# Two stick-breaking heads side by side on the array, and three small jobs handed to GpSimd

## The chip, the core and the metric

The kernel runs on one core of one Trainium2 chip. The metric is the device time of one execution in microseconds (us), as the median of several runs. The core has five queues that run on their own and meet through semaphores: TensorE (PE, matrix products), VectorE (DVE), ScalarE (ACT), GpSimd (POOL) and SyncE (SP, which issues most loads). Each executes its instructions strictly in the order in which they were built.

## What is computed

The reference is one layer of a hybrid decoder for 256 tokens of width 2048. The change touches the token mixer, the first of three sub-layers. The mixer projects its input once and splits the result into three groups:

- a diagonal state space model (S5) over 512 channels,
- eight stick-breaking attention heads of 64 channels,
- sixteen NSA attention heads (compressed, selected and window keys) that share a relative position bias.

Stick-breaking, cut to what matters:

```python
z = einsum('bqhd,bkhd->bhqk', qb, k) * scale
log1m = where(mask, log_sigmoid(-z), 0.0)
later = cumsum(log1m, axis=3, reverse=True) - log1m
w = where(mask, exp(log_sigmoid(z) + later), 0.0)
o = einsum('bhqk,bkhd->bqhd', w, v)
```

After the mixer come cross-attention into 256 memory tokens and a gated MLP; both are left as they are.

## The kernel before, in words

All matrices are float32. A weight chunk of 128x1024 (512 KB) is loaded by SP into one of four buffers `raw` (L270), rounded into `hi` by ACT (L291), and the remainder `lo` is taken by DVE (L292); three buffers of each. TensorE then makes three products per block, hi and lo of the weights with hi and lo of the activations (L306 to L308, or L314 to L316 where the activations are the stationary side), into PSUM tiles `pj`, of which there are three. This stream of projection products fills TensorE from one end of the program to the other, and everything else is woven into it.

The order is made when the program is built: a list scheduler takes instructions by a priority (`lane`) and by a time that it reckons itself, and writes one fixed order per engine. S5 (`s5_work`) is a background generator that is advanced while weight chunks are asked for (`weights`, L265 to L280); its 16 scan states live in the tiles `Ec` and `Es`, their inputs `pb` and outputs `pa` are TensorE products, and most of its work is DVE's (all at L190 in the trace, the line of a helper).

The places that the change and the prediction speak of:

- `stick_breaking` (L790 to L836). Four tiles of two heads. Per head: two products of k and q into a PSUM tile `mx` (L814, L815; head 0 in partitions 0 to 63, head 1 in 64 to 127), two bf16 products that add the mask (L817, L818), Abs, Exp and Ln on ACT (L821 to L823), softplus on DVE (`sbs`, L824), two products with triangular and full matrices that make the running sum (L825, L826), Exp on ACT (L829), and two products with v into one half of the PSUM tile `op` (L830, L832). After both heads ACT and DVE take `op` as hi and lo (L834, L835).
- `nsa_compress` (L855 on) follows; its 32 products of `kv` (L877) end in a Gelu on ACT (`hid`, L885), whose function table is another one than that of Exp and Ln. `nsa_values` and `nsa_keys` are further projections.
- `s5_out` ends S5 with a Gelu (L765) and a gate of four products (`s5zs`, exponentials at L782).
- `nsa_slab` (L951 to L962) loads the bias as a tile `slab` of 128x16x256 (2 MB) from DRAM in eight loads, issued by ACT. `slab` takes the memory of `Es`, so the loads wait for the end of S5.
- `nsa` (L974 on) clears two constants' tiles by DVE: `pc` (L989, 128x1024) and `tcs` (L992, two of 128x60). The first reader of `slab` is L1015 on DVE; the products of the queries `nq` with the keys are L1011 and L1012.

Of the kernel before, what the change touches and what calls it, by code (L numbers as in the profile page):

```python
# [8 lines left out]
F32 = mybir.dt.float32  # L9
F32R = mybir.dt.float32r  # L10
ACTF = mybir.ActivationFunctionType
# [14 lines left out]
BIG = 1e30  # L26
# [138 lines left out]
class Parts:  # L165
# [9 lines left out]
    def range(self, k, n):  # L175
        if k == 0 and self.first is not None:
            assert n == 1
            return self.first
        return self.tiles[k // self.n][:, k % self.n:k % self.n + n]
# [18 lines left out]
class Program:  # L198
# [47 lines left out]
    def after(self, ins, other):  # L246

        self.tc.add_manual_dep(ins.ins, other.ins.name, mybir.DependencyInfo(
            mybir.DependencyClass.NoSync, mybir.DependencyReason.DATA), reason="issue order")

    def exp_ln_table(self, others):

        ins = self.nc.scalar.preload_act_table_set("natural_log_exp_and_others")
        for o in others:
            self.after(ins, o)
        return ins
# [252 lines left out]
    def mixer(self):  # L509
# [6 lines left out]
        with ExitStack() as nsa:  # L516
            self.nsq = pool(nsa, "nsq", 1)
            self.slabp = pool(nsa, "slabp", 1)
            with ExitStack() as s5:
                self.s5p = pool(s5, "s5p", 1, "right")  # L520
                self.s5w = pool(s5, "s5w", 2, "right")
                self.s5_tables()
                self.load_x()
                with ExitStack() as st:
                    self.sbp = pool(st, "sbp", 1)
                    self.sbw = pool(st, "sbw", 2)
                    self.stick_breaking()
                self.nsk = pool(nsa, "nsk", 1)
                self.nsa_compress()
                self.nsa_values()  # L530
                self.s5_out()
            self.resp = pool(self.ctx, "resp", 1, "right")
            self.R = self.resp.tile([128, 2, D], F32, name="R")
            self.mixq = pool(self.ctx, "mixq", 1, "right")
            self.mix += [self.mixq.tile([128, 4, 2, 256], F32R, name=f"mix{i}")
                         for i in range(2, 4)]
            with ExitStack() as st:
                self.nsp = pool(st, "nsp", 1, "right")
                self.nsw = pool(st, "nsw", 2, "right")
                self.nsa_slab()  # L540
                self.nsa_queries()
                self.nsa()
# [248 lines left out]
    def stick_breaking(self):  # L791
        nc, a, V, S = self.nc, self.a, self.nc.vector, self.nc.scalar
        q = self.sbp.tile([128, 4, 256], F32, name="sbq")
        k = self.sbp.tile([128, 4, 256], F32, name="sbk")
        v = self.sbp.tile([128, 2, 512], F32, name="sbv")
        for i, ps in enumerate(self.to_cols(a["win_sv"][0], self.X, 512, 2, 0, KD)):
            S.copy(v[:, i, :], ps)
        while len(self.sins) < 4:
            self.step()
        table = self.exp_ln_table(self.sins)  # L800
        for t in range(4):
            ps = self.to_rows(a["win_c"], t, self.X)
            S.activation(q[:, t, :], ps, ACTF.Copy, scale=HD ** -0.5)
            ps = self.to_rows(a["win_c"], 4 + t, self.X)
            V.tensor_copy(k[:, t, :], ps)
        self.nsa_bias()
        mm = nc.tensor.matmul
        for t in range(4):
            ops = self.op.tile([128, 512], F32, name="op")
            for hh in range(2):  # L810
                rows = slice(64 * hh, 64 * hh + 64)
                h = 2 * t + hh
                z = self.mx.tile([128, 512], F32, name="mx")
                mm(z[:, 0:256], k[rows, t, 0:128], q[rows, t, :], start=True, stop=False)  # L814
                mm(z[:, 256:384], k[rows, t, 128:256], q[rows, t, 128:256], start=False,  # L815
                   stop=False)
                mm(z[:, 0:128], self.ident16, self.smask16, start=False, stop=False)  # L817
                mm(z[:, 256:384], self.ident16, self.smask16, start=False, stop=True)  # L818
                e = self.sbw.tile([128, 384], F32, name="sbe")
                sp = self.sbw.tile([128, 384], F32, name="sbs")  # L820
                S.activation(e, z[:, :384], ACTF.Abs)  # L821
                self.after(S.activation(e, e, ACTF.Exp, scale=-1.0), table)
                S.activation(e, e, ACTF.Ln, bias=1.0)  # L823
                V.scalar_tensor_tensor(sp, z[:, :384], 0.0, e, ALU.max, ALU.add)  # L824
                mm(z[:, 0:384], self.ntri, sp, start=False, stop=False, skip_group_check=True)  # L825
                mm(z[:, 128:256], self.nones, sp[:, 256:384], start=False, stop=True,  # L826
                   skip_group_check=True)
                w = self.sbw.tile([128, 384], F32, name="sbe")
                S.activation(w, z[:, :384], ACTF.Exp)  # L829
                mm(ops[rows, 0:256], v[:, 0, 64 * h:64 * h + 64], w[:, 0:256],  # L830
                   start=True, stop=False)
                mm(ops[rows, 128:256], v[:, 1, 64 * h:64 * h + 64], w[:, 256:384],  # L832
                   start=False, stop=True)
            S.copy(self.mix[1][:, t, 0, :], ops[:, :256])  # L834
            V.tensor_sub(self.mix[1][:, t, 1, :], ops[:, :256],  # L835
                         self.mix[1][:, t, 0, :].bitcast(F32))  # L836
# [114 lines left out]
    def nsa_slab(self):  # L951


        g_dr, n = self.g_dr, 128 // SKEW

        self.nq = self.nsp.tile([128, 8, 2, 256], F32R, name="nq")
        self.slab = self.slabp.tile([128, NH, 256], F32, name="slab", tag="Es")
        with self.lane("first"):
            for c in range(n):
                src = bass.AP(g_dr.tensor, g_dr.offset + 127 - c,  # L960
                              [[384 - n, SKEW], [SKEW * 384, NH], [1, 256]])
                self.nc.scalar.dma_start(self.slab[c:128:n], src)  # L962

    def nsa_queries(self):
        a, V, S, q = self.a, self.nc.vector, self.nc.scalar, self.nq
# [8 lines left out]
    def nsa(self):  # L974
        nc, a, V, S = self.nc, self.a, self.nc.vector, self.nc.scalar
        p, mm = self.nsp, nc.tensor.matmul
        vcb, vv, gate, ks, q = self.vcb, self.vv, self.gate, self.ks, self.nq
# [6 lines left out]
        def qcol(h):  # L984
            return 4 * (h // 8) + 2 * (h // 4 % 2) + h % 2


        pc = p.tile([128, 2, NH, 32], F32, name="pc")
        V.memset(pc, 0.0)  # L989
        tcs = [p.tile([128, 2, 4, NC_], F32, name=f"tcs{i}") for i in range(2)]  # L990
        for t in tcs:
            V.memset(t[:, 0], BIG)  # L992
        halves = lambda t: t.rearrange("p (c k) -> p c k", c=2)
        for quad in range(4):
            o = self.pq.tile([128, 2, 256], F32, name="pa")
            start = [None, None]
            for b in range(2):
                n = 128 if b else 128 + NK
                for gl in range(2):
                    h0, v = 4 * quad + 2 * gl, 4 * b + 2 * (quad // 2) + gl  # L1000
                    sums = self.nsw.tile([128, 2, 2], F32, name="sums")
                    pes, pts = [], []
                    for r in range(2):
                        h = h0 + r
                        kh, kl = (k[:, h // 8, gl].rearrange("p c n -> p (c n)") for k in ks[b])
                        t = qcol(h)
                        z = self.mx.tile([128, 512], F32, name="mx")

                        for qt, m in enumerate((256, n + 128)):
                            qs, zs = slice(128 * qt, 128 * qt + 128), z[:, qt * n:qt * n + m]  # L1010
# [35 lines left out]
                    for c, (k0, k1) in enumerate(((0, 256), (256, 384))):  # L1046
                        for r, pt in enumerate(pts):
                            ins = mm(o[64 * r:64 * r + 64, gl, 128 * c:256], vv[:, c, v, :],  # L1048
                                     pt[:, k0:k1], start=start[r] is None, stop=False,
                                     skip_group_check=True)  # L1050
# [285 lines left out]
```

## Time and profile before

| | us |
|---|---|
| median of three runs | 1294.0 (1293.86 to 1295.22) |
| the profiled execution, its own time | 1293.79 |
| its span, first to last instruction | 1292.0 |
| TensorE busy | 1254.6 (97%) |
| VectorE busy | 883.8 (68%) |
| ScalarE busy | 659.9 (51%) |
| GpSimd busy | 13.3 (1%) |
| mean granted TensorE clock | 0.992 |

The clock is a share of the higher of TensorE's two levels (2.4 GHz); 0.5 is the lower one. Start times are counted from the first instruction. A matrix product's shown duration contains its way through the array, so that products that follow each other closely overlap in the rows; what a product occupies is the distance from its start to the next one's. "Idle before" names who ended a wait.

### The profile page before, as it was taken

The numbers are of one execution on the slowest core, as the hardware profiler recorded it, in microseconds if no ns is written. First come the engines' busy times: TensorE is split into PE (matmuls) and PEld (weight loads), VectorE is DVE, ScalarE is ACT, GpSimd is POOL, SyncE is SP. The second block draws the span as 40 slices with busy tenths as digits, with TensorE's granted clock in tenths as the row PEclk, the third lists the DMA queues.
The fourth block names the chain that finished last, engine by engine and source line by source line (L and its number), as shares of the span: only waits on it lengthen the run. The fifth ranks groups of instructions, "written<-read, shape, count | busy, mean of one in ns | idle before, by whom it ended". The sixth has DMA issues, their size and how long they took to land.

```text
span 1292.0 us, 23010 instructions
## 1 busy us (share of the span) xinstructions
PE 1254.6 (97%) x9222; PEld 1160.8 (90%) x9222; DVE 883.8 (68%) x1510; ACT 659.9 (51%) x1032; POOL 13.3 (1%) x23
## 2 busy tenths in 40 slices
PE   7999999999999999899999999999999999999996
PEld 7788898988779899799999999999999988888896
DVE  7799896877765675776666666666666654544557
ACT  6884434666554355455555555555555543334342
POOL 0200000000000000000000000000000000000000
PEclk9999999999999999999999999999999999999998
DMA  8653348633447564445555565565655755656573
GB/s 306 192 167 128 99 137 224 186 117 103 131 168 279 189 208 151 137 142 194 192 192 195 196 195 191 191 193 194 196 196 190 254 193 195 195 184 199 187 228 130
DMA packets 68886, 237.37 MB, mean 184 GB/s; under 512 B 7787, under 2 KB 10652, under 8 KB 68012
## 3 DMA queue, kind: packets, MB, share of 16 engines
q1 hardware_dynamic: 64720, 230.21, 53.7%
q10 hardware_dynamic: 3276, 3.47, 1.2%
q0 software_dynamic: 784, 2.23, 0.9%
q8 instruction: 72, 1.18, 0.4%
q14 instruction: 34, 0.28, 0.1%
HBM read 231.82 MB, written 2.49 MB: 181 GB/s over the span
## 4 chain that ended last, share of the span: by engine, by line
PE 76%; DVE 3%; ACT 1%; issue 1%; DMA 0%; DVEq 0%; ACTq 0%
PE pj L306 14%; PE pj L307 14%; PE pj L308 14%; PE pj L314 9%; PE pj L316 9%; PE pj L315 9%; PE pa L1048 2%; DVE lo L292 1%; PE mx L1011 1%; PE mx L1012 1%; DVE R L1144 1%; DVE R L1149 1%; PE op L1041 0%; PE pb L1041 0%; ACT hi L291 0%
## 5 line engine op out<-in xcount | busy, mean ns | idle before, releaser
L292 DVE TENSOR_TENSOR lo<-raw,hi 128x1024 fp32r<-128x1024 f32 (+2 forms) x403 | 488.5, 1212 | 339.0 <-ACT hi L291 337.9
L291 ACT CAST hi<-raw 128x1024 fp32r<-128x1024 f32 (+2 forms) x403 | 419.8, 1042 | 510.7 <-PE pj L307 276.4
L307 PE MATMUL pj<-mix,hi 128*128 128x256 f32 x1380 | 381.9, 277 | 0.0
L306 PE MATMUL pj<-mix,hi 128*128 128x256 f32 x1380 | 381.1, 277 | 0.0
L308 PE MATMUL pj<-mix,lo 128*128 128x256 f32 x1380 | 381.0, 276 | 0.0
L307 PEld LDWEIGHTS pj<-mix,hi 128*128 128x128 f32 x1380 | 259.2, 188 | 0.1
L308 PEld LDWEIGHTS pj<-mix,lo 128*128 128x128 f32 x1380 | 259.2, 188 | 0.1
L306 PEld LDWEIGHTS pj<-mix,hi 128*128 128x128 f32 x1380 | 259.1, 188 | 0.2
L306 PE MATMUL pj<-A,hi 128*128 128x256 f32 x496 | 141.2, 288 | 8.6 <-ACT hi L291 8.6
L308 PE MATMUL pj<-A,lo 128*128 128x256 f32 x496 | 139.2, 288 | 4.2 <-DVE lo L292 4.0
L307 PE MATMUL pj<-A,hi 128*128 128x256 f32 x496 | 140.4, 286 | 0.0
L306 PEld LDWEIGHTS pj<-A,hi 128*128 128x128 f32 x496 | 95.9, 194 | 11.2 <-ACT hi L291 9.3
L308 PEld LDWEIGHTS pj<-A,lo 128*128 128x128 f32 x496 | 94.6, 194 | 8.1 <-DVE lo L292 5.6
L307 PEld LDWEIGHTS pj<-A,hi 128*128 128x128 f32 x496 | 96.1, 194 | 1.9 <-issue 1.9
L315 PE MATMUL pj<-lo,act 128*128 128x512 f32 (+1 forms) x280 | 96.8, 347 | 0.0
L316 PE MATMUL pj<-hi,act 128*128 128x512 f32 (+1 forms) x280 | 96.8, 347 | 0.0
L315 PE MATMUL pj<-lo,A 128*128 128x512 f32 (+2 forms) x288 | 96.3, 336 | 0.0
L316 PE MATMUL pj<-hi,A 128*128 128x512 f32 (+2 forms) x288 | 95.6, 333 | 0.0
L314 PE MATMUL pj<-hi,A 128*128 128x512 f32 (+2 forms) x288 | 91.0, 334 | 0.0
L314 PE MATMUL pj<-hi,act 128*128 128x512 f32 (+1 forms) x280 | 89.7, 347 | 0.0
L315 PEld LDWEIGHTS pj<-lo,A 128*128 128x128 f32 x288 | 54.1, 188 | 6.5 <-issue 1.1
L315 PEld LDWEIGHTS pj<-lo,act 128*128 128x128 f32 x280 | 52.9, 189 | 6.6
(324 smaller groups left out, 1809.5 us busy)
## 6 DMA issues: line engine op xcount, KB each, us to landing
raw<-in_w_up SPq DMA_DIRECT2D x176, 512.0 KB, 4.2
raw<-in_w_down SPq DMA_DIRECT2D x92, 512.0 KB, 3.3
raw<-in_win_c SPq DMA_DIRECT2D x48, 512.0 KB, 3.9
raw<-in_w_out SPq DMA_DIRECT2D x32, 512.0 KB, 4.0
raw<-in_win_sv SPq DMA_DIRECT2D x8, 512.0 KB, 4.7
raw<-in_wk_m SPq DMA_DIRECT2D x8, 512.0 KB, 4.9
raw<-in_wv_m SPq DMA_DIRECT2D x8, 512.0 KB, 4.2
raw<-in_wq SPq DMA_DIRECT2D x8, 512.0 KB, 4.1
```

Of the source, the lines that this page charges most:

```text
L291: self.last_hi = nc.scalar.copy(hi[:, :n], raw[:, :n])
L292: self.last_lo = nc.vector.tensor_sub(lo[:, :n], raw[:, :n], hi[:, :n].bitcast(F32))
L306: mm(ps, hi, ah, start=start, stop=False)
L307: mm(ps, hi, al, start=False, stop=False)
L308: self.last_mm = mm(ps, lo, ah, start=False, stop=stop)
L314: mm(ps, ah, hi, start=start, stop=False)
L315: mm(ps, ah, lo, start=False, stop=False)
L316: self.last_mm = mm(ps, al, hi, start=False, stop=stop)
L1011: mm(zs, q[:, t, gl, qs], kh[:, 0:m], start=True, stop=False)
L1012: mm(zs, q[:, t, gl, qs], kl[:, 0:m], start=False, stop=True)
L1048: ins = mm(o[64 * r:64 * r + 64, gl, 128 * c:256], vv[:, c, v, :], pt[:, k0:k1], start=start[r] is None, stop=False, skip_group_check=True)
L1144: ins = V.scalar_tensor_tensor(r, r, mean, self.gb[:, 0, c0:c1], ALU.subtract, ALU.mult)
```

## The change

The two heads of a tile are now built together. Their four products of k and q form one row on TensorE (head 0, head 1, head 0, head 1), each pair on the upper and lower 64 rows of the array; the mask products follow. Their four products with v form another row, head by head on the two 64-column halves. `in_row` fixes that order for the scheduler, and ties the first product of a tile to the last of the tile ahead. The first product with v waits for the second head's Exp as well. The eight loads of `slab` are issued by GpSimd instead of ACT, and GpSimd writes `pc` and `tcs` instead of DVE.

```diff
+    def in_row(self, row):
+        for ins, other in zip(row[1:], row):
+            self.after(ins, other)
...
-            for hh in range(2):
-                rows = slice(64 * hh, 64 * hh + 64)
-                h = 2 * t + hh
-                z = self.mx.tile([128, 512], F32, name="mx")
-                mm(z[:, 0:256], k[rows, t, 0:128], q[rows, t, :], start=True, stop=False)
-                mm(z[:, 256:384], k[rows, t, 128:256], q[rows, t, 128:256], start=False,
-                   stop=False)
-                mm(z[:, 0:128], self.ident16, self.smask16, start=False, stop=False)
-                mm(z[:, 256:384], self.ident16, self.smask16, start=False, stop=True)
+            halves = [slice(64 * hh, 64 * hh + 64) for hh in range(2)]
+            zs = [self.mx.tile([128, 512], F32, name="mx") for _ in halves]
+            row = []
+            for c in range(2):
+                for z, rows in zip(zs, halves):
+                    row.append(mm(z[:, 256 * c:384 if c else 256],
+                                  k[rows, t, 128 * c:128 * c + 128], q[rows, t, 128 * c:256],
+                                  start=c == 0, stop=False))
+            for z in zs:
+                row.append(mm(z[:, 0:128], self.ident16, self.smask16, start=False, stop=False))
+                row.append(mm(z[:, 256:384], self.ident16, self.smask16, start=False, stop=True))
+            self.in_row(values[-1:] + row)
+            ws, exps = [], []
+            for z in zs:
...
-                S.activation(w, z[:, :384], ACTF.Exp)
-                mm(ops[rows, 0:256], v[:, 0, 64 * h:64 * h + 64], w[:, 0:256],
-                   start=True, stop=False)
-                mm(ops[rows, 128:256], v[:, 1, 64 * h:64 * h + 64], w[:, 256:384],
-                   start=False, stop=True)
+                exps.append(S.activation(w, z[:, :384], ACTF.Exp))
+                ws.append(w)
+            row = values = []
+            for c, (k0, k1) in enumerate(((0, 256), (256, 384))):
+                for hh, (w, rows) in enumerate(zip(ws, halves)):
+                    h = 2 * t + hh
+                    row.append(mm(ops[rows, 128 * c:256], v[:, c, 64 * h:64 * h + 64], w[:, k0:k1],
+                                  start=c == 0, stop=c == 1))
+            self.tc.add_manual_dep(row[0].ins, exps[1].ins.name, mybir.DependencyInfo(
+                mybir.DependencyClass.Sync, mybir.DependencyReason.DATA), reason="side by side")
+            self.in_row(row)
...
-                self.nc.scalar.dma_start(self.slab[c:128:n], src)
+                self.nc.gpsimd.dma_start(self.slab[c:128:n], src)
...
-        V.memset(pc, 0.0)
+        nc.gpsimd.memset(pc, 0.0)
...
-            V.memset(t[:, 0], BIG)
+            nc.gpsimd.memset(t[:, 0], BIG)
```

The scheduler makes a new order of all that stands around these instructions. Three places of it follow. The changed kernel's lines are 4 higher ahead of `stick_breaking` (L310 for L306) and 16 higher behind it (L893 for L877).

**The end of stick-breaking.** TensorE around the last product with v. Before (`sbs` are the products of the running sum, L830 and L832 those with v, L877 the compression):

```order
L308 MATMUL pj<-A,lo 128x256
L825 MATMUL mx<-sbs,cst 128x384
L826 MATMUL mx<-sbs,cst 128x128
L306 MATMUL pj<-A,hi 128x256
L307 MATMUL pj<-A,hi 128x256
L877 MATMUL mx<-kv,raw 128x75 x9
L190 MATMUL pb<-s5us,s5lb 128x256 x2
L877 MATMUL mx<-kv,raw 128x75
L190 MATMUL pa<-Ec,s5c 32x256
L830 MATMUL op<-sbe,sbv 64x256
L832 MATMUL op<-sbe,sbv 64x128
L877 MATMUL mx<-kv,raw 128x75 x6
```

and now:

```order
L190 MATMUL pb<-s5us,s5lb 128x256 x2
L835 MATMUL mx<-sbs,cst 128x384
L836 MATMUL mx<-sbs,cst 128x128
L190 MATMUL pa<-Ec,s5c 32x256
L893 MATMUL mx<-kv,raw 128x75 x16
L190 MATMUL pb<-s5us,s5lb 128x256 x2
L190 MATMUL pa<-Ec,s5c 32x256
L835 MATMUL mx<-sbs,cst 128x384
L836 MATMUL mx<-sbs,cst 128x128
L318 MATMUL pj<-hi,A 128x256
L845 MATMUL op<-sbe,sbv 64x256 x2
L845 MATMUL op<-sbe,sbv 64x128 x2
```

ACT at the same place now (L831 to L833 are Abs, Exp, Ln of the last head, L839 its last Exp, L901 the Gelu):

```order
L831 ACTIVATE sbe<-mx 128x384
L832 ACTIVATE sbe<-sbe 128x384
L833 ACTIVATE sbe<-sbe 128x384
L885 COPY kv<-pj 64x256 x2
L901 ACT_TABLE_LOAD
L901 ACTIVATE hid_1887<-mx,pb_1885 128x4x15
L295 CAST hi<-raw 128x1024
L885 COPY kv<-pj 64x256
L839 ACT_TABLE_LOAD
L839 ACTIVATE sbe<-mx 128x384
L295 CAST hi<-raw 128x1024
L850 CAST mix_97<-op 128x256
```

The sixteen `kv` products used to stand on both sides of the last products with v; now all of them stand ahead, and one projection product is left between the last running sum and the products with v. On ACT the Gelu has come ahead of the last Exp, which takes two more table loads (before, all eight Exp stood ahead of the Gelu).

**The end of S5.** DVE around the last state (`Es<-s5m`). Before:

```order
L190 SCALAR_TENSOR_TENSOR s5z<-s5v_121,s5z 128x256 x2
L292 TENSOR_TENSOR lo<-raw,hi 128x1024
L190 TENSOR_TENSOR s5m_2031<-s5z,Ec 128x512
L190 TENSOR_TENSOR s5m_2032<-s5z,Es 128x512
L292 TENSOR_TENSOR lo<-raw,hi 128x1024
L190 TENSOR_TENSOR Ec<-s5m_2031,s5m_2032 128x256
L190 SCALAR_TENSOR_TENSOR Es<-s5m_2031,s5m_2032 128x256
```

and now:

```order
L190 SCALAR_TENSOR_TENSOR s5z<-s5v_121,s5z 128x256 x2
L296 TENSOR_TENSOR lo<-raw,hi 128x608
L190 TENSOR_TENSOR s5m_2031<-s5z,Ec 128x512
L190 TENSOR_TENSOR s5m_2032<-s5z,Es 128x512
L296 TENSOR_TENSOR lo<-raw,hi 128x608
L190 TENSOR_TENSOR Ec<-s5m_2031,s5m_2032 128x256
L190 SCALAR_TENSOR_TENSOR Es<-s5m_2031,s5m_2032 128x256
```

S5 ends earlier in the stream: behind the 52nd weight chunk on DVE instead of the 57th, and on TensorE its last outputs stand behind 998 products into `pj` instead of 1085.

**The bias.** ACT before:

```order
L938 CAST kh_2091<-pj 64x2x128 x2
L962 DMA slab<-g_dr 16x16x256 x8
L291 CAST hi<-raw 128x1024 x2
L938 CAST kh_2091<-pj 64x2x128 x2
L765 ACTIVATE s5u<-s5u 128x1024
```

GpSimd now:

```order
L947 MEMSET kl_2092 128x1152
L947 MEMSET kl_2544 128x1024
L978 DMA slab<-g_dr 16x16x256 x8
L1005 MEMSET pc 128x1024
L1008 MEMSET tcs_3328 128x60
L1008 MEMSET tcs_3329 128x60
```

The eight loads have left ACT's queue, and nothing on GpSimd stands behind them but the clearing of `pc` and `tcs`.

## Rows read from the trace of the kernel before

**Rows 1.** Busy time by window: S5 and stick-breaking, then up to the first NSA product.

```profile
core 0: us, PE busy (x) PEld busy (x) DVE busy (x) ACT busy (x) POOL busy (x), PEclk, DMA share, GB/s
89.60:210.80 121.20, 121.20 (x901) 106.44 (x900) 112.58 (x200) 51.44 (x88) 2.56 (x3) 1.00 0.44 140
210.80:259.50 48.70, 43.06 (x348) 41.12 (x346) 34.45 (x52) 27.84 (x45) 0.00 (x0) 0.96 0.73 198
```

**Rows 2.** Who waited for whom, 205 to 272 us: total, times, longest.

```profile
DVE lo L292 <- ACT hi L291: 12.0, 6, 8.8
ACT hi L291 <- DMA slab<-g_dr: 9.0, 1, 9.0
PE mx L1011 <- DVE nq L971: 3.0, 1, 3.0
```

**Rows 3.** ACT in order of time: start, length; ACTq is its queue issuing loads.

```profile
214.40 9.10 ACTq L962 DMA_DIRECT2D slab<-g_dr  x8
```

**Rows 4.** Busy time by window where TensorE idles; columns as in rows 1.

```profile
222.00:230.00 8.00, 5.00 (x27) 4.59 (x27) 3.68 (x6) 6.32 (x9) 0.00 (x0) 0.79 1.12 202
232.00:238.00 6.00, 3.48 (x28) 3.10 (x27) 5.33 (x8) 5.03 (x11) 0.00 (x0) 1.00 0.71 224
258.00:268.00 10.00, 7.02 (x47) 6.83 (x46) 8.17 (x34) 5.46 (x18) 0.00 (x0) 0.83 0.42 142
```

**Rows 5.** DVE in order of time, ahead of the first NSA scores.

```profile
256.03 0.91 DVE L989 MEMSET pc<- 128x1024 f32 x1 [0.16 <-DVE lo L292]
256.90 0.18 DVE L992 MEMSET tcs<- 128x60 f32 x2
...
259.31 0.29 DVE L1015 CUSTOM_DVE_ANT_0 tt<-mx,slab 128x128 f32<-128x128 f32 x1
```

**Rows 6.** TensorE in order of time: one head's products with k and q.

```profile
80.58 0.70 PE L814 MATMUL mx<-sbq,sbk 64*128 64x256 f32 x2
...
81.43 0.23 PE L817 MATMUL mx<-m,m 128*128 128x128 bf16 x1
```

**Rows 7.** The same view: one head's products with v, and what follows.

```profile
97.28 0.65 PE L830 MATMUL op<-sbe,sbv 128*64 128x256 f32 x2
...
98.07 0.70 PE L814 MATMUL mx<-sbq,sbk 64*128 64x256 f32 x2
```

**Rows 8.** The same view in NSA: two heads' products with v, and what follows.

```profile
274.07 0.86 PE L1048 MATMUL pa<-pt,vv 128*64 128x256 f32 x6
274.86 0.38 PE L1011 MATMUL mx<-kh,nq 128*128 128x256 f32 x1
```

**Rows 9.** The same view at the end of S5: projections, then the first last output.

```profile
212.88 0.28 PE L308 MATMUL pj<-A,lo 128*128 128x256 f32 x1
212.99 0.28 PE L306 MATMUL pj<-A,hi 128*128 128x256 f32 x1
213.10 0.28 PE L307 MATMUL pj<-A,hi 128*128 128x256 f32 x1
213.31 0.40 PE L190 MATMUL pa<-Ec,s5c 128*32 128x256 f32 x1
```

**Rows 10.** DVE in order of time: S5's last state, and two remainders together.

```profile
210.36 0.42 DVE L190 SCALAR_TENSOR_TENSOR Es<-s5m,s5m 128x256 f32<-128x256 f32 x1
...
224.67 2.36 DVE L292 TENSOR_TENSOR lo<-raw,hi 128x1024 fp32r<-128x1024 f32 x2 [8.78 <-ACT hi L291]
```

**Rows 11.** ACT's only load of the Gelu table (L885): shortest/median/longest ns, first and last.

```profile
L885 ACT ACT_TABLE_LOAD  x1: 1283/1283/1283, 167.1 to 167.1; - x1
```

**Rows 12.** The loads that GpSimd issues (L496): ns as in rows 11, then landing.

```profile
L496 POOL DMA_DIRECT2D s5us<-Ec x12: 550/551/693, 35.4 to 42.5; - x12
...
DMA to landing us min/median/max: 3.3/5.3/8.8
```

**Rows 13.** Busy time by window while GpSimd issued those loads; columns as in rows 1.

```profile
20.00:40.00 20.00, 18.84 (x134) 17.00 (x134) 17.44 (x40) 15.88 (x28) 4.60 (x9) 1.00 0.79 265
```

**Rows 14.** DMA, 214 to 232 us: bytes and share by queue, issues with time to landing.

```profile
q10 hardware_dynamic: 2176, 2.10, 65.0%
...
slab<-g_dr ACTq DMA_DIRECT2D x8, 256.0 KB, 10.3
raw<-in_win_c SPq DMA_DIRECT2D x3, 512.0 KB, 6.7
```

More of the change, by code (lines that the diff above doesn't have):

```diff
@@ L806, in stick_breaking @@
         self.nsa_bias()
-        mm = nc.tensor.matmul
+        mm, values = nc.tensor.matmul, []
         for t in range(4):
             ops = self.op.tile([128, 512], F32, name="op")
-            for hh in range(2):
-                rows = slice(64 * hh, 64 * hh + 64)
-                h = 2 * t + hh
-                z = self.mx.tile([128, 512], F32, name="mx")
-                mm(z[:, 0:256], k[rows, t, 0:128], q[rows, t, :], start=True, stop=False)
-                mm(z[:, 256:384], k[rows, t, 128:256], q[rows, t, 128:256], start=False,
-                   stop=False)
-                mm(z[:, 0:128], self.ident16, self.smask16, start=False, stop=False)
-                mm(z[:, 256:384], self.ident16, self.smask16, start=False, stop=True)
+            halves = [slice(64 * hh, 64 * hh + 64) for hh in range(2)]
[12 more added lines that the diff above has]
+            for z in zs:
                 e = self.sbw.tile([128, 384], F32, name="sbe")
```

## The prediction

> **What bounds the kernel now.** I read first the busy time by window, then who waited for whom, then the engines in order of time. From 89.6 to 210.8 us, the stretch of stick-breaking and S5, TensorE is busy in all 121.2 us, and DVE is close behind with 112.58 [rows 1]. In the next 48.7 us TensorE loses 5.6 us of busy time and some clock [rows 1]. The reader is to see two things there: TensorE is the bound nearly everywhere, so only its own work and its holes count, and DVE is so near that work taken from TensorE in the first stretch may not show.
>
> The holes have names. ACT's longest wait in this part is 9.0 us for `slab` [rows 2]: it spends 214.40 to 223.50 issuing eight loads [rows 3], and every cast to `hi` stands behind them. DVE, which needs `hi`, waits 8.8 us in one piece [rows 2]. TensorE has three finished chunks, uses them up, and idles 8.00 - 5.00 = 3.0 us between 222 and 230; the granted clock of that window is 0.79, because TensorE comes back from the hole at the lower level, 1.2 GHz, for a time, and that is another 8 x 0.21 = 1.7 us [rows 4]. Between 232 and 238 it idles 2.5 us more while ACT and DVE work off what piled up [rows 4]. A second hole is at the first NSA product: 10.00 - 7.02 = 3.0 us, and 10 x 0.17 = 1.7 us of clock behind it [rows 4], 3.0 of it a wait for DVE's `nq` [rows 2]. DVE clears `pc` and `tcs` just there [rows 5].
>
> **The change part by part**, against the profiled execution (1293.8; the median is 0.2 above it).
>
> *The rows of products: TensorE's work.* One head's products with v occupy 98.07 - 97.28 = 0.79 us [rows 7]. NSA's products have the same shape on two 64-column halves, built head by head, and two heads take 274.86 - 274.07 = 0.79 us [rows 8]: the second head is free. Four tiles save 4 x 0.79 = 3.2 us. One head's products of k and q occupy 81.43 - 80.58 = 0.85 us [rows 6]. No row shows two 64-row halves beside each other; below, they save nothing (nothing is added, so a loss is excluded but for a few tens of ns per switch), above, 4 x 0.85 = 3.4. I take 3.4, by the nearest row, the column halves. Sum 6.6 us of work.
>
> The Trainium skill, "TensorE: Matmul & The Clock Gate", section on packing small matmuls, states that four row tiles measured 3.07 times faster than one after the other. At that efficiency (0.77) two halves would be 1.54 times faster, an estimate that makes the 3.4 a 2.4. No run shows it yet.
>
> *What DVE and the new waits take back.* S5's last outputs stand 87 projection products earlier on TensorE than before. A projection product occupies 0.11 us (212.88, 212.99, 213.10 [rows 9]), so that TensorE would reach them at 213.3 - 9.8 - 6.6 = 196.9. But they need S5's last state from DVE, done at 210.8 before [rows 10], and DVE's queue ahead of it has become shorter by only five remainders, four of 2.36 / 2 = 1.18 [rows 10] and a short one of some 0.7 (608 of 1024 columns): 5.4 us. DVE, busy for 112.6 us of the stretch [rows 1], then needs 107.2 from 89.6 on, which is 196.8. Both arrive at once, if neither ever waits for the other. Before, DVE waited 121.2 - 112.6 = 8.6 us of the stretch [rows 1]. If it waits as long as before, S5 ends at 205.4 and TensorE stands 8.5 us; if it never waits, nothing is lost. I take 4.0, about the middle, since most of DVE's waits were for casts that TensorE's own pace held up. In this lies the new wait at the last tile. ACT there casts (about 1.0), copies (0.4), loads a table (1.28 [rows 11]) and takes the Exp (0.5) behind the Gelu, some 3.2 us, while TensorE has about 1.9 us of S5 products, running sum and one projection; it stands for 1 to 2 us before the products with v. DVE works on S5 meanwhile, so this is not added. Net of both parts: 6.6 - 4.0 = 2.6 gained, between 6.6 and -1.9.
>
> *The bias by GpSimd.* The loads leave ACT, and with them the hole (3.0 + 1.7 = 4.7) and the backlog (2.5). The backlog's wait is at the gate of S5, where ACT also has casts of keys, so that some of it may stay. I take 6.2, between 4.7 and 7.2. GpSimd pays: its loads took 0.55 us each to issue [rows 12], 8 x 0.55 = 4.4 us, and it has nothing else to do. Issued from about 201 on, and landing in the 10.3 us that they took before [rows 14], they are there by 216; the first reader comes at 259.3 now [rows 5], at some 248 after. That cover is 30 us.
>
> The loads then compete with the weights, which did not flow while ACT stood. The 2.10 MB took 65.0% of 18 us of all DMA engines, 11.7 us, and weight loads beside them took 6.7 us to land [rows 14]. A chunk is used about every 2.7 us (24 products at 0.113), and four buffers `raw` mean that a load is asked for up to 10.9 us ahead: then it costs nothing. At the other end the weights wait for all that does not fit: 1.79 MB of them took 35.4% of 18 us, 6.4 us [rows 14], so a chunk of 0.52 MB takes 1.9 of every 2.7 us, in 20 us some 6 are free, and 11.7 - 6 = 5.7 come late. I take 1.0, as the weight loads that did run beside `slab` landed inside the 10.9.
>
> *The clearing by GpSimd.* DVE spends 0.91 + 0.18 us directly ahead of the NSA scores [rows 5], so 1.1 is sure as long as DVE is late there. It is late because it stood 8.8 us in the hole before. With that gone it has 34.45 us of work in 48.7 [rows 1], plus the 5.4 of remainders moved there. I take 3.0, between 1.1 and the whole 4.7. On GpSimd the clearing stands behind the loads and takes about 1 us, covered by the same cushion.
>
> Sum: 2.6 + 6.2 + 3.0 - 1.0 = 10.8, and 1293.8 - 10.8 = **1283.0**. Everything behind 268 us keeps its work; the NSA stage ends some 60 products later in the stream, but still ahead of the second half of the output projection, its first reader.
>
> **The rivals.** *TensorE's holes move into the first stretch.* DVE and ACT become the bound there: the rows of products bring -1.9, the wait at the last tile makes the clock fall once more (-1.7, as in rows 4), and the two later holes give only 4.7 and 1.1, less 1.0 for the DMA. That is 1.2 gained, 1292.6. For it speaks that DVE has 8.6 us of slack in 121 [rows 1], against it that this slack was mostly TensorE's doing. Chance 0.13.
>
> *The bias comes too late: slower.* `slab` has one reader that matters, DVE at the first NSA score, and behind it in DVE's queue stand the remainders that TensorE needs. If GpSimd's eight loads went one after the other, each with the 8.8 us of its slowest landing [rows 12], the last would land at 201 + 70 = 271, 23 us after the reader at 248. TensorE has three chunks in hand, 8 us, and would stand 15: 1283.0 + 15 = 1298. It decides against the change from 5.9 us per load on (47 us for eight). Against it: twelve such loads were issued 0.55 us apart, without waiting for landings [rows 12], while DVE was busy for 17.44 of 20 us [rows 13]. Chance 0.05. The Trainium skill, "SBUF — State Buffer", in the paragraph on the "DVE blocks DMA" trap, has a rule of this kind: a load issued by GpSimd can starve while DVE runs an instruction that uses both of its ports, as GpSimd cannot write the descriptors, and the load should be issued by ACT or SP. By that rule the time would be this rival's; rows 12 and 13 do not bear it out at their density.
>
> *The 64-row halves do not overlap*, so that the change does only half of what it says: 3.4 less of TensorE's work, of which DVE's limit hides a part. That makes 1283.0 + 2.0 = 1285, up to 1286.4. No row speaks for or against. Chance 0.12.
>
> **How the numbers follow.** The forecast as described has 0.70, with a range of its own of 1278 to 1289 from the bounds above (all at their best 1275.3, all at their worst 1295.6, neither likely). A difference of under 0.2% (2.6 us) can hardly be told from none. Faster is the forecast, the third rival, and four tenths of the first: 0.87. Same is most of the rest of the first: 0.07. Slower is the late bias and a little of the first: 0.06. The range for 8 in 10 is 1277 to 1292, which takes in the halves that do not overlap and most of the first rival's way.
>
> **What would show it.** Right: no wait of ACT for `slab`; TensorE's holes up to S5's end about 4 us in all; two heads' products with v in 0.8 us and those of k and q in about 0.85; S5's last state on DVE between 197 and 205; a short or no hole at the first NSA product; GpSimd's loads 0.55 us apart. Wrong: TensorE waiting for DVE's remainders or for `raw` from 200 to 240, which would be the DMA engines; a wait of DVE for `slab`; or lower clock between 150 and 210 us.

## The result and the profile after

The changed kernel takes **1285.4 us** (median of 4 runs, 1283.6 to 1287.0), the kernel before on the same chip 1293.9 (1293.8 to 1295.2): a ratio of 0.9931, 95% interval 0.9914 to 0.9949, so 8.5 us faster. The forecast was 1283.0 within 1277 to 1292. The profiled execution took 1286.6, its span 1284.4.

First the windows that answer to [rows 1, 4], with a new one at stick-breaking's last tile (160 to 182); columns as there.

```profile
89.60:207.00 117.40, 114.13 (x857) 98.94 (x856) 111.00 (x201) 52.08 (x84) 2.87 (x4) 0.97 0.43 134
207.00:256.00 49.00, 47.41 (x403) 46.39 (x402) 37.52 (x57) 31.89 (x54) 5.31 (x11) 1.00 0.80 231
160.00:182.00 22.00, 18.76 (x118) 15.22 (x118) 20.02 (x39) 9.56 (x16) 2.13 (x3) 0.84 0.41 130
222.00:230.00 8.00, 7.05 (x58) 6.49 (x57) 4.14 (x5) 5.33 (x10) 0.00 (x0) 1.00 0.96 285
232.00:238.00 6.00, 5.65 (x44) 5.15 (x43) 5.83 (x10) 4.45 (x9) 0.00 (x0) 1.00 0.75 252
250.00:265.00 15.00, 15.00 (x131) 14.87 (x131) 14.24 (x51) 11.54 (x31) 1.12 (x3) 1.00 0.55 176
```

The two old holes are nearly gone: 8.00 - 7.05 = 0.95 and 6.00 - 5.65 = 0.35 idle, at full clock, and nothing at NSA's start. A new one stands where TensorE was busy in every microsecond before: 22.00 - 18.76 = 3.2 us idle, and 22 x 0.16 = 3.5 us of clock. TensorE in order of time shows its two pieces, and ACT in order of time what made them.

```profile
166.51 0.39 PE L318 MATMUL pj<-hi,A 128*128 128x256 f32 x1 [1.43 <-ACT hi L295]
168.71 1.55 PE L845 MATMUL op<-sbe,sbv 128*64 128x256 f32 x8 [1.81 <-ACT sbe L839]
```

```profile
163.92 1.28 ACT L901 ACT_TABLE_LOAD   x1
165.21 0.31 ACT L901 ACTIVATE hid<-mx,pb 128x60 f32<-128x60 f32 x1
165.42 1.03 ACT L295 CAST hi<-raw 128x1024 fp32r<-128x1024 f32 x1
166.48 0.37 ACT L885 COPY kv<-pj 64x256 f32<-64x256 f32 x1
166.87 1.28 ACT L839 ACT_TABLE_LOAD   x1
168.16 0.49 ACT L839 ACTIVATE sbe<-mx 128x384 f32<-128x384 f32 x1
```

The last `w` of stick-breaking (an Exp) is now needed later than the compression's first Gelu is issued. So ACT loads the Gelu table, then the Exp table again, and the weight cast and the Exp, for both of which TensorE waits, stand behind the loads. The record of the products with v, at the lower clock after that, is 1.55 us long, where that of the third tile, undisturbed, is 0.87. All that TensorE idles from 89.6 to 207 (117.40 - 114.13 = 3.3 us) is these two pieces, and it waits for ACT in both. The same view of the third tile shows the rows of products at work:

```profile
129.45 0.87 PE L845 MATMUL op<-sbe,sbv 128*64 128x256 f32 x8
130.25 0.92 PE L820 MATMUL mx<-sbq,sbk 64*128 64x256 f32 x8
131.10 0.23 PE L824 MATMUL mx<-m,m 128*128 128x128 bf16 x1
```

Two heads take 0.80 us with v and 0.855 with k and q (0.85 in the rounded rows), which is what one head took [rows 6, 7]. The answers to [rows 2, 14] (waits of 205 to 256 us, then the loads' line) are the last two readings:

```profile
DVE lo L296 <- ACT hi L295: 11.3, 7, 3.1
ACT hi L295 <- DMA raw<-in_win_c: 8.5, 4, 2.9
...
PE pj L312 <- DVE lo L296: 0.9, 2, 0.8
```

```profile
L978 POOL DMA_DIRECT2D slab<-g_dr x8: 562/562/591, 206.7 to 210.6; - x8
...
DMA to landing us min/median/max: 6.5/10.5/15.8
```

ACT waits for `slab` no more, but 8.5 us for weights, of which TensorE feels 1.3.

**Where the 8.5 us come from.** I cut both traces at the start of the same projection products (there are 8,352 in each) and add up in each stretch TensorE's idle time between records, and the time lost to the clock (half of the time at 1.2 GHz). The rest is counted as work. In us, before / after:

| from product to product | time | idle | clock | rest | gained |
|---|---|---|---|---|---|
| start to 300th | 70.0 / 72.1 | 8.9 / 11.0 | 1.7 / 0 | 59.4 / 61.1 | -2.0 |
| to 1,380th (ahead of the first NSA product) | 187.0 / 181.3 | 7.4 / 6.5 | 1.7 / 3.4 | 177.9 / 171.4 | 5.7 |
| to 1,920th (NSA done) | 139.4 / 134.6 | 3.0 / 0 | 1.7 / 0 | 134.7 / 134.6 | 4.8 |
| to the last | 884.4 / 885.3 | 7.2 / 6.5 | 1.7 / 3.4 | 875.5 / 875.4 | -0.9 |

The first and the last row are code that the change does not touch; up to the 300th product the profiles of all kernels here lie between 70.0 and 72.1, whatever was changed behind it. The second row holds the rows of products, 6.5 us less work (171.7 when the same kernel is run again, so a few tenths are uncertain); the idle time hardly falls, as the last tile's 3.2 and 1.3 for late weights took the place of the slab hole; and the clock falls for longer than before. The third row is the hole at NSA's first product, idle and clock [rows 4].

### The profile page after: what moved, and what is told of

It is laid out like the page before. It is cut to its first block, busy times and chain, and to the rows that moved or that the text cites. A ratio compares the mean times of both kernels' runs of the same rounds, so it can differ in the third digit from the quotient of the medians.

```text
span 1284.4 us, 23040 instructions
## 1 busy us (share of the span) xinstructions
PE 1249.5 (97%) x9222; PEld 1155.4 (90%) x9222; DVE 881.2 (69%) x1507; ACT 664.0 (52%) x1034; POOL 18.9 (1%) x34
## 4 chain that ended last, share of the span: by engine, by line
PE 89%; DMA 4%; DVE 3%; ACT 3%; issue 1%; POOL 0%; SPq 0%; ACTq 0%; DVEq 0%
PE pj L310 17%; PE pj L312 17%; PE pj L311 17%; PE pj L318 10%; PE pj L320 10%; PE pj L319 10%; DMA raw<-in_win_u 2%; PE pa L1064 2%; DMA s5us<-Ec 1%; DMA raw<-in_win_c 1%; ACT hi L295 1%; DVE lo L296 1%; PE pa L190 1%; PE mx L893 1%; PE mx L1027 1%
## 5 line engine op out<-in xcount | busy, mean ns | idle before, releaser
L310 PE MATMUL pj<-mix,hi 128*128 128x256 f32 x1380 | 381.9, 277 | 0.0
L310 PEld LDWEIGHTS pj<-mix,hi 128*128 128x128 f32 x1380 | 259.7, 188 | 0.2
L310 PE MATMUL pj<-A,hi 128*128 128x256 f32 x496 | 139.7, 284 | 7.9 <-ACT hi L295 7.2
L311 PE MATMUL pj<-A,hi 128*128 128x256 f32 x496 | 137.8, 281 | 0.0
L310 PEld LDWEIGHTS pj<-A,hi 128*128 128x128 f32 x496 | 93.7, 190 | 11.1 <-ACT hi L295 8.2
L311 PEld LDWEIGHTS pj<-A,hi 128*128 128x128 f32 x496 | 93.8, 190 | 1.2 <-issue 1.2
L318 PEld LDWEIGHTS pj<-hi,A 128*128 128x128 f32 x288 | 54.1, 190 | 7.6 <-ACT hi L295 1.6
```

What stands on the lines that cost most here:

```text
L310: mm(ps, hi, ah, start=start, stop=False)
L311: mm(ps, hi, al, start=False, stop=False)
L318: mm(ps, ah, hi, start=start, stop=False)
```

## The experiments

Each is timed against the kernel before on the same chip. That took 1294.0 us beside experiments 1 and 2 and 1295.0 to 1295.1 beside the others, on other chips, so that across this line ratios compare better than microseconds. Theory 1 is the reading above: the rows pay in full, and ACT's table loads eat them. The rival is the prediction's: DVE takes the rows' work back.

**1. The parts alone.** Three kernels, each the kernel before with one part of the change. Rows alone:

> Only the rows of products; bias loads stay on ACT and the clearing on DVE. Theory 1 (from the trace after the change): the rows save 6.6 us of TensorE's work and the new wait at the last tile, 3.2 us of idle and 3.4 us of clock behind it, takes 6.6 back: no gain, 1293 to 1295, with a hole of some 3 us and a lower clock at the last tile's values. Theory 2 (the prediction's): DVE gives back 4.0, a gain of 2.6: 1291.3.

Bias alone:

```
-                self.nc.scalar.dma_start(self.slab[c:128:n], src)
+                self.nc.gpsimd.dma_start(self.slab[c:128:n], src)
```

> Only the eight bias loads by GpSimd. Both theories: the hole at 222 goes (3.0 idle, 1.7 clock, 2.5 backlog). Theory 1 (trace after): 7.2 less some 1.4 of late weights = 5.8, 1288. Prediction's terms: 6.2 less 1.0 = 5.2, 1288.7. If part of the hole at the first NSA product was the heritage of the slab hole, its 3.0 idle and 1.7 clock go too, or most of it: 1283.5 to 1286.

Clearing alone:

```
-        V.memset(pc, 0.0)
+        nc.gpsimd.memset(pc, 0.0)
...
-            V.memset(t[:, 0], BIG)
+            nc.gpsimd.memset(t[:, 0], BIG)
```

> Only the clearing of pc and tcs by GpSimd. Theory 1: DVE is late at the first NSA score because it stood behind the bias loads, so that without the clearing it is just 1.1 us (0.91 + 0.18) less late: gain 1.1, 1292.8, and a hole of 1.9 with its clock drop stays. Theory 2: the clearing alone makes the hole: gain 3.0 to 4.7, 1289 to 1291.

Measured: rows 1289.2 (ratio 0.9964, 0.9951 to 0.9976), bias 1287.9 (0.9957, 0.9945 to 0.9970), clearing 1290.9 (0.9969, 0.9958 to 0.9980). By these ratios that is 4.7, 5.6 and 4.0 us: 14.3 in sum where the whole change brings 8.9 by its own. So they share something, and neither theory had said what. Cut in the same way, the rows alone win 1.5 in the second stretch (theory 1: none) and 3.5 in NSA; the bias alone 2.0 and 3.5; the clearing alone loses 0.6 and wins 5.0. **Each of the three takes the hole at NSA's first product away.** DVE in order of time, shows why; first the kernel before, with TensorE's wait behind it, then the one with the bias alone, in which DVE still clears, then the rows alone:

```profile
257.39 0.75 DVE L971 SCALAR_TENSOR_TENSOR nq<-pj,nq 64x256 fp32r<-64x256 f32 x2
...
261.16 0.29 DVE L1015 CUSTOM_DVE_ANT_0 tt<-mx,slab 128x128 f32<-128x128 f32 x1
...
261.90 0.43 DVE L971 SCALAR_TENSOR_TENSOR nq<-pj,nq 64x256 fp32r<-64x256 f32 x1
```

```profile
262.48 0.36 PE L1011 MATMUL mx<-kh,nq 128*128 128x256 f32 x1 [2.98 <-DVE nq L971]
```

```profile
255.14 0.75 DVE L971 SCALAR_TENSOR_TENSOR nq<-pj,nq 64x256 fp32r<-64x256 f32 x2
...
257.17 0.42 DVE L971 SCALAR_TENSOR_TENSOR nq<-pj,nq 64x256 fp32r<-64x256 f32 x1
257.63 0.29 DVE L1015 CUSTOM_DVE_ANT_0 tt<-mx,slab 128x128 f32<-128x128 f32 x1
```

```profile
254.24 0.91 DVE L1005 MEMSET pc<- 128x1024 f32 x1 [0.16 <-PE pj L311]
...
257.64 0.42 DVE L987 SCALAR_TENSOR_TENSOR nq<-pj,nq 64x256 fp32r<-64x256 f32 x1
258.10 0.29 DVE L1031 CUSTOM_DVE_ANT_0 tt<-mx,slab 128x128 f32<-128x128 f32 x1
```

Before, the scheduler had put the second tile's `nq` behind the scores of two heads, and TensorE waited for it until 262.48. With each of the three edits it puts at least one piece of that `nq` ahead of the first score. The rows-alone kernel has both old suspects still in place, the hole behind ACT's loads (TensorE idles 3.8 us in 205 to 225) and DVE's clearing, and yet no hole at NSA (0.2 us). So I read the hole as one of order and not of lateness, and my reading of it for the clearing alone (1.1) fell. No run moved that one instruction alone, so this is read from the rows and not shown by itself.

The bias alone also shows the other side of that edit. Its slab hole is gone, but ACT then waits for weights, and TensorE for ACT, 3.35 us (the ACT row first, then TensorE's):

```profile
231.97 1.04 ACT L291 CAST hi<-raw 128x1024 fp32r<-128x1024 f32 x1 [4.92 <-DMA raw<-in_win_c]
```

```profile
234.33 0.58 PE L306 MATMUL pj<-s5zs,hi 128*128 128x256 f32 x1 [3.35 <-ACT s5z L782]
```

**2. The Gelu behind the last Exp.** The changed kernel, with one more issue order on ACT:

```
             self.in_row(row)
+            self.last_exp = exps[1]
...
                                ACTF.Gelu_apprx_tanh, bias=pb)
+            self.after(act, self.last_exp)
             self.gelus.append(act)
```

> The changed kernel, with the first Gelu of the compression held behind the last Exp of stick-breaking on ACT, so that no table is loaded ahead of that Exp. Theory 1: the wait at the last tile (1.4 + 1.8 us idle, 3.4 us clock) came from the two table loads and goes whole: 6.6 less, 1279, as far as DVE (118.6 us busy of 125) lets TensorE have it: 1279 to 1281. Theory 2 (the prediction's): DVE is the bound of this stretch, and TensorE waits for S5's last state instead, so that less than 2 us come: 1283.5 to 1285.

Measured 1282.5 (0.9917, 0.9902 to 0.9932), between the two. In the profile the Exp comes first and the wait shrinks from 3.2 to 1.7 us (three pieces), at full clock:

```profile
165.37 0.49 ACT L839 ACTIVATE sbe<-mx 128x384 f32<-128x384 f32 x1
165.88 1.28 ACT L902 ACT_TABLE_LOAD   x1
```

From the 300th projection product to the 1,140th it is 3.3 us faster than the changed kernel. But this profiled execution took 1286.6 (the other four 1282.1 to 1282.8) and loses more than that between 215 and 240 us, where ACT waits 10.0 us for weights. So the wait at the tile is one thing, and the weights behind the bias loads another.

**3. Spread loads.** The kernel of experiment 2, each of the eight bias loads held behind one cast of a weight chunk:

```
             self.last_hi = nc.scalar.copy(hi[:, :n], raw[:, :n])
+            if self.slabs:
+                self.slabs.pop(0)(self.last_hi)
...
+            def go(cast):
+                with self.lane("first"):
+                    ins = self.nc.gpsimd.dma_start(self.slab[c:128:n], src)
+                self.tc.add_manual_dep(ins.ins, cast.ins.name, mybir.DependencyInfo(
+                    mybir.DependencyClass.Sync, mybir.DependencyReason.DATA), reason="spread")
```

> The kernel with the Gelu behind the last Exp, and each of the eight bias loads held behind one cast of a weight chunk, so that they go out one per 0.5 MB of weights. Theory 1: what is left of the hole from 215 to 240 (ACT waits 10.0 us for weights in that kernel's profile, TensorE idles 3.5 us in five pieces and loses 1.7 of clock) is made by the eight loads that go out within 4 us: it goes, 1278 to 1281, and runs spread less. Theory 2: the weights are late for want of buffers or by their own number: the same 2.1 MB delay them as much when spread, 1282 to 1283.5.

Measured **1279.6** (1278.7 to 1281.3; 0.9883, 0.9869 to 0.9896), the fastest of all. GpSimd in order of time, two of its eight loads; then 215 to 240 us by window, in the profile of experiment 2 and in this one:

```profile
218.94 0.56 POOL L987 DMA_DIRECT2D slab<-g_dr  x1 [1.93 <-ACT hi L295]
221.66 0.56 POOL L987 DMA_DIRECT2D slab<-g_dr  x1 [2.16 <-ACT hi L295]
```

```profile
215.00:240.00 25.00, 21.48 (x160) 20.29 (x159) 16.02 (x22) 14.01 (x25) 0.00 (x0) 0.93 0.76 230
```

```profile
215.00:240.00 25.00, 24.39 (x211) 24.01 (x210) 19.31 (x28) 16.20 (x27) 3.36 (x6) 1.00 1.01 267
```

The same 2.1 MB, 2.7 us apart, cost TensorE 0.6 us of idle there instead of 3.5 and 1.75 of clock, and ACT has no wait for weights left in this profile. The pair shows more than the medians do, as the profile of experiment 2 is that of the 1286.6; between the medians it is 2.9, by the ratios 4.4. Two other pairs below go the same way: 1286.1 against 1284.0 without rows, 1285.2 against 1284.1 with the Gelu early, where the intervals overlap. The burst made the greater part, but not all: in three later kernels with spread loads (experiments 5, 7 and the second of 6) ACT still waits 4.7 to 7.4 us for weights between 205 and 245, and TensorE idles 0.6 to 2.1 us between 215 and 240, against 1.6 to 3.5 in the six profiles with a burst by GpSimd.

**4. No rows.** First without the rows, with bias and clearing by GpSimd; then the same with spread loads.

> The kernel before with the bias loads and the clearing by GpSimd, and no rows of products. Theory 1: the rows' 6.6 us are eaten whole by the wait at the last tile, so that this kernel is as fast as the changed one: 1284 to 1286.5. Theory 2 (the prediction's): the rows bring 2.6 net, so that it is slower by that: 1287 to 1288.5.

> No rows of products, bias loads spread over the casts, clearing by GpSimd: beside the spread kernel (1279.6) it leaves out the rows and the Gelu's new place alone. Theory 1: the rows are worth 6.6 us of TensorE's work less what still stands at the last tile there (0.8 + 0.5 idle, 1.7 clock) = 3.6: 1283 to 1284. Theory 2 (DVE takes the rows' work back): within 1.5 of it, 1279.5 to 1281.

Measured 1286.1 (0.9935, 0.9923 to 0.9948) and 1284.0 (0.9917, 0.9902 to 0.9933). The first cannot be told from the changed kernel, run beside it again at 1285.2 (0.9923, 0.9910 to 0.9937):

> The changed kernel itself, beside the others on one chip: 1284 to 1287 by either theory. Which of its runs lie near 1284 and which near 1287 is not told by any; if the profile shows a hole at 215 to 240 that the first profile does not have, the weights behind the bias loads make the spread.

The sign that was named there is missing: between 215 and 240 us this profile idles 2.0 us and the first one 1.6. What makes the spread of the changed kernel stays open.

In the second kernel without rows, with the loads spread, leaving the rows out costs 4.4 us against 1279.6, and the intervals do not meet. The traces have 3.6 of it in the second stretch (180.3 against 176.7), with no wait at the last tile in the kernel without rows. Theory 1 had said 3.6, the rival under 1.5.

**5. The Gelu early again**, in the spread kernel, with the rows:

> The spread kernel with the Gelu back ahead of the last Exp, as in the changed kernel. Theory 1: the wait of 3.2 us idle and 3.4 of clock is back in place of 3.0: 3.6 slower, 1283 to 1284, as without rows. Theory 2 (DVE sets the end of the stretch, and the wait is taken from its cover): within 1.5, 1279.5 to 1281.

Measured 1284.1 (0.9913, 0.9898 to 0.9927): 4.4 slower than with the Gelu late, and the same as without any rows. (In the traces' second stretch it is 178.7, between the spread kernel's 176.7 and the 180.3 without rows; 1.4 of these 2.0 lie at the last tile and 0.6 at late weights, and the clock loses 1.7 in both kernels.) The wait is back in its old form:

```profile
166.27 0.39 PE L320 MATMUL pj<-hi,A 128*128 128x256 f32 x1 [1.43 <-ACT hi L295]
168.47 0.87 PE L848 MATMUL op<-sbe,sbv 128*64 128x256 f32 x8 [1.81 <-ACT sbe L842]
```

**6. Is it the neighbourhood that makes two halves overlap?** The kernel of experiment 2, the products of k and q head by head within their row:

```
-            for c in range(2):
-                for z, rows in zip(zs, halves):
+            for z, rows in zip(zs, halves):
+                for c in range(2):
```

> The kernel with the Gelu behind the last Exp, but the products of k and q head by head in their row, so that just one of four neighbours lies on the other half. Theory 1: two 64-row halves overlap fully (0.855 us for both heads in the trace) and TensorE is the bound, so that a second head costs again 0.6 to 0.85 us in each of four tiles: 2.4 to 3.4 slower than with the row, 1285 to 1286. Theory 2: DVE is the bound there, and the time is the same within 1 us.

Measured 1282.8 (0.9911, 0.9895 to 0.9928), no slower. That looks like theory 2, but TensorE says otherwise: the eight records still take 131.09 - 130.23 = 0.86 us.

```profile
130.23 0.93 PE L820 MATMUL mx<-sbq,sbk 64*128 64x256 f32 x8
131.09 0.23 PE L824 MATMUL mx<-m,m 128*128 128x128 bf16 x1
```

So this edit did not undo the overlap. The next does, in the spread kernel: each head's two mask products (whole array) stand between the heads.

> The spread kernel with each head's two mask products (whole array) right behind its products of k and q, so that they stand between the two heads. Theory 1: the whole-array products stop the overlap, the pair takes about 1.7 instead of 0.86 us in four tiles, and TensorE is the bound: 3.4 slower, 1282.5 to 1283.5. Theory 2: overlap stays, or DVE hides it: 1279 to 1280.5.

```profile
131.06 0.92 PE L823 MATMUL mx<-sbq,sbk 64*128 64x256 f32 x4
131.91 0.23 PE L826 MATMUL mx<-m,m 128*128 128x128 bf16 x1
...
132.13 0.92 PE L823 MATMUL mx<-sbq,sbk 64*128 64x256 f32 x4
132.98 0.23 PE L826 MATMUL mx<-m,m 128*128 128x128 bf16 x1
```

Each head takes its 0.85 us again, and the time is 1284.1 (0.9917, 0.9902 to 0.9932): 4.4 slower, of which 4 x 0.85 = 3.4 are that. In the trace's second stretch it is 2.9: 5.5 more of work, less 1.0 of idle and 1.7 of clock, as the wait at the last tile shrinks. The work beyond 3.4 is not explained; the new order also puts S5's products between the products of one head in the second tile. DVE does not hide the work that is put back, so TensorE is the bound there.

**7. The clearing back on DVE**, in the spread kernel:

> The spread kernel with pc and tcs cleared by DVE again. Theory 1: the hole at the first NSA product came from DVE being late, and DVE is no longer late: no difference, 1279 to 1280.5. Theory 2 (the prediction's): the clearing itself costs 1.1 to 3.0 there: 1280.7 to 1282.6, with a hole at the first NSA product.

Measured 1282.2 (0.9901, 0.9885 to 0.9916). The medians stand 2.6 apart, as theory 2 says, but the intervals overlap, and the hole it named is not there: TensorE is busy in all of 250 to 265.

```profile
250.00:265.00 15.00, 15.00 (x124) 14.03 (x124) 14.57 (x60) 11.74 (x32) 0.00 (x0) 1.00 0.43 145
```

In the second stretch this profile loses 1.3: at the last tile it is 0.9 faster, as the clock does not fall there, and then it loses 2.3, with two pieces of idle (0.5 and 1.6 us, up to 228.5 and 231.7) where ACT waits for weights and DVE has not cleared yet (it does at 247.3). The stretch of NSA (1,380th to 1,920th product) is 0.9 longer, and there the kernels agree: the three that clear on DVE and have no hole (rows alone, bias alone, this one) take 135.5 to 135.9 us for it, the ten profiles in which GpSimd clears 134.4 to 134.8. So the clearing itself costs about the 1.1 us that DVE spends on it; whether the rest of the 2.6 hangs on it stays open.

**Up to the end of S5, by trace.** At the 1,100th product into `pj` all of stick-breaking and S5 lies behind in every kernel, and nothing of the bias is felt yet (but in the rows-alone kernel, whose loads stand earlier; it is left out). From the 300th product to there, in us:

| kernels | time | idle | clock |
|---|---|---|---|
| no rows (before; bias, clearing alone; both of experiment 4) | 146.1 to 146.2 | 1.8 | 0 |
| rows, Gelu early (the change; again; experiment 5) | 146.2; 146.3; 144.9 | 4.9 to 5.0 | 3.4; 3.4; 1.7 |
| rows, Gelu late, clock falls (experiments 3 and 6, the first) | 143.5; 143.6 | 3.5 | 1.7 |
| rows, Gelu late, clock stays (experiments 2 and 7) | 142.9; 142.6 | 3.8 | 0 |
| masks between the heads, Gelu late, clock stays (6, the second) | 145.3 | 2.6 | 0 |

The five kernels without rows lie within 0.02 us. So in the changed kernel the rows gain nothing up to here (it is 0.05 and 0.15 us behind), all of the 5.7 of the second stretch comes behind it, with the bias, and with the Gelu late the rows gain 2.6 to 3.6.

## Why the prediction was right, and where not

**The rows' work, 6.6: right, the unseen half too.** The k-and-q term was taken from the column halves, 3.4, and the trace gives 0.855 us for two heads against 0.85 for one. The third rival (no overlap) is out; so is the 2.4 worked out from the packing rule of the Trainium skill, "TensorE: Matmul & The Clock Gate". The same section's other rule, that a further tile adds about 4 ns to the span of one, is of the size of what this trace shows, 6 to 7 ns more for two heads than for one. By the cut up to the 1,100th product the work saved is 6.5 us in the changed kernel and 5.3 to 6.5 in the seven profiles with full rows.

**What DVE and the new waits take back, 4.0: the wrong mechanism, and too little.** The failing step is "DVE works on S5 meanwhile, so this is not added". The wait at the last tile was foreseen, with the table load and a length of 1 to 2 us, and then booked as free because DVE was held to be the bound. It is 3.2 us, since the weight cast stands behind the Gelu's table load as well, and the clock falls after it, which the prediction charged only to its first rival. Together 6.7 against 6.5 of work, so that the net of the rows was about 0 and not 2.6: 146.2 us against 146.1 up to the 1,100th product. Experiments 4, 5 and 6 show it: without the early Gelu the rows are worth 4.4 (3.6 in the traces), with it nothing (1.6 in the traces, where the clock fell for less), and 3.4 us of TensorE's work put back cost 4.4 (1.7 to 2.7 in the traces up to the 1,100th product). The sign that the prediction named for "wrong", a lower clock between 150 and 210, is what the profile has. S5's last state did come at 202.8 on DVE, within the 197 to 205 named, but that says nothing on what bounds the stretch: DVE's 111.0 busy of 117.4 us was a near bound, not the bound. The holes of about 4 us that the forecast looked for up to S5's end are there too, 3.3 us, but by luck: TensorE waited in them for ACT, not for S5.

**The bias, 6.2 less 1.0 for the DMA: right in sum, wrong in its parts.** The hole and the backlog gave their whole 7.2, and late weights took 1.3 at 222 to 238 in the profile of the changed kernel. That DMA term was the least certain (0 to 5.7), and rightly: between 215 and 240 us the changed kernel's profile idles 1.6, and the five other profiles with the same eight loads in a burst 2.0 to 3.5, three of them (experiments 1, 2 and the first of 4) with a fall of the clock behind. Spreading them gave 2.9 of the medians (1282.5 to 1279.6), and 2.1 and 1.1 in the two other pairs.

**The clearing, 3.0: the hole went whole, 4.8, but not for that reason.** The step "It is late because it stood 8.8 us in the hole before" is the one that failed: the rows-alone kernel has the hole behind the loads and none at NSA. By the rows of experiment 1 the order of `nq` and scores made it, and each of the three edits changes that order. What the clearing costs by itself is the 1.1 of the lower bound. In the whole change it is gained once, whichever edit gets the credit.

**The sum**: 10.8 forecast; from the 300th product to the end of NSA 5.7 + 4.8 = 10.5 in the profile. That this is close is luck: two errors nearly cancelled, 2.6 too much for the rows and 1.8 too little for the clearing. The 2.0 at the start and 0.9 at the layer norm, in code that is the same, bring that profile to 7.6.

**The other rivals.** The first had the right place and the fall of the clock, but not the late stretches, which kept their whole gain. The late bias did not happen: the last load was issued at 210.6 and no load took over 15.8 us, so all were there by 227, and DVE's first score read `slab` at 255.4. The rule of the Trainium skill, "SBUF — State Buffer", on the "DVE blocks DMA" trap is not tested here: the eight loads went out 0.56 us each, but from 206.9 to 210.8 DVE ran one subtraction of 1.22 us and idled for 2.7, and no row shows which of its instructions use both ports.

## What to carry to other kernels

When work is taken from the bounding engine, the instructions that fed it keep their order on their own engines, and some come behind a neighbour that was harmless before: look at every table load, cast and load between the last two users, and price the wait with the clock that falls after it. An engine at 95% is not yet the bound; put the work back where only the other engine feels it, and see. Parts that each remove the same hole cannot be summed, and a hole that goes with each of three unrelated edits points to the order, not to an operation.

Of what is left in the fastest kernel, 1.7 us idle at the last tile (0.80 for a cast, 0.52 for the Exp, 0.34 for a remainder) and 22 x 0.08 = 1.8 us of clock were not tried.

## What the hardware showed unexpectedly

Two heads on opposite 64-row halves overlap though all products of one were issued ahead of the other's (0.863 us for both, against 0.855 interleaved); whole-array products between them stopped it (0.85 us for each head, 1.06 from head to head).

Eight loads of 256 KB issued by GpSimd in 4.5 us made the weight loads of 512 KB beside them late. The weight loads that ran between the first issue and the last landing of the eight took 8.4 to 10.5 us on average and 11.1 to 14.3 at most in the six profiles with this burst, against 4.1 to 4.3 ahead of the bias loads in the kernel before. With the same loads 2.7 us apart it was 6.5 to 8.0 on average and 9.0 to 11.4 at most, in five profiles.

The same two waits, 1.43 and 1.81 us, cost the clock 22 x 0.16 = 3.5 us in the changed kernel and 22 x 0.08 = 1.8 in the kernel of experiment 5: the granted clock was 0.84 and 0.92 in 160 to 182 us, the lower level being 1.2 GHz in both. Nor was the wait's length what told them apart: 0.69, 0.52 and 0.47 us left the clock alone in experiment 2, and 0.80, 0.52 and 0.34 made it fall in experiment 3.
